# Differential attention: both maps' scores in one five-bank tile, a second transpose bank, and a third of each block's halves taken out of PSUM by ScalarE and VectorE

## The chip, the cores and the metric

The kernel runs on one core of one Trainium2 chip. The metric is the device time of one launch in microseconds, median of several runs. TensorE (PE) multiplies and transposes into PSUM, VectorE (DVE) and ScalarE (ACT) read PSUM and SBUF, GpSimd (POOL) works on SBUF here, and SyncE (SP) issues the DMAs. [...]

## The reference, cut to what matters

One step of a two-layer backbone. Layer 0 mixes tokens by differential attention: 8 heads, each with two maps of width 64, 1024 latent queries against 1280 keys (256 cached and 1024 new).

```
s = jnp.einsum('bqhmd,bkhmd->bhmqk', qi, k).astype(jnp.float32) * scale
p = jax.nn.softmax(s, axis=-1)
a = p[:, :, 0] - lam * p[:, :, 1]
return jnp.einsum('bhqk,bkhe->bqhe', a.astype(v.dtype), v)
```

The projections before it, the output projection, the feed-forward parts and all of layer 1 are as they were.

## The kernel before, in words

The changed part is the stage of latent differential attention, `diff_attention`, about 13% of the span. It works on 32 pairs: one head and two blocks of 128 queries. Every matrix product is made of halves (a rounded high part and the rest), so that fp32 accuracy comes out of three cheaper products. For a pair, with block i (0 or 1) and map m (0 or 1), a step is a method with one letter:

- S: six matmuls put a block's 128 x 1280 scores of one map into PSUM. R: VectorE's maximum over them. E: ScalarE's exponential of them, with their sum.
- c: two small VectorE operations on the sums of both maps. C: VectorE's combination `a` of both exponentials.
- T: transposes of `a`, in groups g of 4, 4 and 2 tiles of 128 keys. V: ScalarE copies a group from PSUM to SBUF (`a32`, two buffers). P: GpSimd rounds the copy to the high half and subtracts for the low half (`aT`).
- A: three matmuls of one tile of 128 keys with V into the accumulator, ten tiles for a pair. X, B, Y: the result is copied out, turned by two transposes and written to DRAM.
- W: a piece of the output projection's weights is split, in every second round (ScalarE, then VectorE).

The order is written out by hand: the string `ROUND` is run once for each pair, `DRAIN` once behind them. A token is letter, g or m, i, and how many rounds ago its pair began: `T201` is step T, group 2, block 0, of the pair before. Each engine runs its own instructions strictly in that order and waits where data or a buffer is missing; the framework puts in the waits, for a tile in PSUM bank by bank: two accesses of one tile by different engines to the same bank are put one behind the other, in the order of the text.

Before, a score tile takes three banks and there are two of them in turn; the transposes of T and B share one bank, and the accumulator has one.

Of the kernel before, what the change touches and what calls it, by code (L numbers as in the profile page):

```python
# [18 lines left out]
P = 128  # L19
# [25 lines left out]
def hybrid_step(ctx: ExitStack, tc: tile.TileContext, x_prompt, x_sample, cache_diff_k, cache_diff_v,  # L45
# [670 lines left out]
    def diff_attention(op, s1_all, wo_pool, pre, kv0, q0):  # L716
        NKB = NCB + 8
        NK = NKB * P
        with sbuf("da") as sb, psum("dap") as ps:
            class Pair:  # L720
# [9 lines left out]

                def step_S(self, m, i):

                    S = self.S[i, m] = ps.tile([P, 3 * 512], F32, name="S", tag="S", bufs=2)
                    for j in range(0, NK, 512):
                        n = min(NK - j, 512)
                        for f in range(2):
                            pe.matmul(S[:, j:j + n], lhsT=self.q[:, f, m, i * P:(i + 1) * P],  # L737
                                      rhs=kv[self.h][0][:, m, j:j + n], start=(f == 0), stop=(f == 1))

                def step_R(self, m, i):  # L740
                    if m == 0:
                        self.nm[i] = sb.tile([P, 2], F32, name="nm", tag="sm", bufs=8)
                        self.s2[i] = sb.tile([P, 2], F32, name="s2", tag="sm", bufs=8)
                    dve.tensor_reduce(out=self.nm[i][:, m:m + 1], in_=self.S[i, m][:, 0:NK], axis=AX.X, op=ALU.max,  # L744
                                      negate=True)

                def step_E(self, m, i):
                    e = self.e[i, m] = sb.tile([P, NK], F32, name="e", tag="e", bufs=4)
                    act.activation(out=e, in_=self.S[i, m][:, 0:NK], func=AF.Exp, bias=self.nm[i][:, m:m + 1],  # L749
                                   accum_out=self.s1(i) if m == 0 else self.s2[i][:, 0:1])  # L750

                def step_c(self, _, i):

                    r = self.s2[i][:, 1:2]
                    dve.reciprocal(out=r, in_=self.s2[i][:, 0:1])
                    dve.scalar_tensor_tensor(out=r, in0=self.s1(i), scalar=neglam, in1=r, op0=ALU.mult, op1=ALU.mult)

                def step_C(self, _, i):

# [3 lines left out]

                def step_T(self, g, i):

                    tp = self.tp[i, g] = ps.tile([P, 4, P], F32, name="tpa", tag="t", bufs=1)
                    for t in range(4 * g, min(4 * g + 4, NKB)):
                        pe.transpose(tp[:, t - 4 * g, :], self.a[i][:, t * P:(t + 1) * P], ident)

                def step_V(self, g, i):  # L770
                    n = min(4, NKB - 4 * g)
                    x = self.a32[i, g] = sb.tile([P, 4, P], F32, name="a32", tag="a32", bufs=2)
                    act.copy(out=x[:, 0:n, :], in_=self.tp[i, g][:, 0:n, :])  # L773

                def step_P(self, g, i):

                    n = min(4, NKB - 4 * g)
                    if g not in self.aT:
                        self.aT[g] = sb.tile([P, 2, 4 if g < 2 else 2, 2 * P], F32R, name="aT",
                                             tag="aT" if g < 2 else "aTb", bufs=4 if g < 2 else 2)  # L780
                    hi, lo = [self.aT[g][:, f, 0:n, i * P:(i + 1) * P] for f in range(2)]
                    x = self.a32[i, g][:, 0:n, :]
                    pool_round(hi, x)
                    (dve if self.last else pool).tensor_tensor(out=lo, in0=x, in1=hi.bitcast(F32), op=ALU.subtract)  # L784
# [16 lines left out]

                def step_B(self, _, __):

                    self.ot = ps.tile([P, 4, P], F32, name="tpo", tag="t", bufs=1)
                    for i in range(2):
                        pe.transpose(self.ot[:, i, :], self.oT[:, i * P:(i + 1) * P], ident)

                def step_Y(self, _, __):
# [2 lines left out]
                    t0 = self.tbs[0] * P  # L811
                    dma(out=o_d[t0:t0 + 2 * P, self.h * P:(self.h + 1) * P].rearrange("(t p) d -> p t d", p=P), in_=ot)

            pairs = [Pair(h, (tb, tb + 1)) for h in range(DH) for tb in range(0, 8, 2)]
            kv = {0: kv0}
            pairs[0].q = q0
# [2 lines left out]
            def wo_piece(i):  # L819
# [5 lines left out]

            ROUND = ("c001 A003 T012 A003 V202 V102 S000 R111 P213 T112 P002 A003 A003 E011 A003 P202 V012 "
                     "C001 P102 E111 T212 R000 V112 W000 S100 P012 R100 T001 X003 A002 V212 c011 E000 A002 "
                     "A002 B003 S010 V001 C011 Y003 T201 R010 A002 P112 E100 A002 T101 S110").split()  # L830


            DRAIN = ("c001 l1 A003 A003 V202 P213 l0 T012 V102 R111 A003 A003 P002 E011 P202 V012 A003 "
# [1167 lines left out]
```

## Time and profile before

| | |
|---|---|
| median of 3 runs | 3202.52 us (3199.64 to 3203.96) |
| the profiled execution, its own time | 3199.07 us |
| its span, first to last instruction | 3197.3 us |
| granted clock of TensorE, mean | 0.981 of full speed |
| busy share of the span | PE 94%, DVE 64%, ACT 44%, POOL 43% |
| the changed stage, first S to the last Y | about 387 to 818 us |

The profile's times count from the span's start. Matmuls overlap in TensorE's pipeline, so a busy share of PE is not a share of its peak. The profiled execution lies 3.45 us below the median of the runs.

### The profile page before, as it was taken

To read this page: it belongs to the slowest core of one execution; us is meant where nothing else is said; L and a number is where in the kernel's file an instruction comes from. 1 tells how busy PE (TensorE), PEld (TensorE's weight loads), DVE (VectorE), ACT (ScalarE), POOL (GpSimd) and SP (SyncE) were. 2 spreads that over 40 slices of the span, in tenths; PEclk is the share of its full clock that TensorE was granted. 3 is DMA by queue.
4 is the path that set the end of the run, shared out by engine and by line. 5 is a ranking of instruction groups with operands and counts; after the bars stand their busy time and mean duration, and the time that the engine had idled before them with its cause. 6 is when DMAs were issued, how large, how long until landed. Compare 5 with 4: busy or idle time off the path is not lost.

```text
span 3197.3 us, 47914 instructions
## 1 busy us (share of the span) xinstructions
PE 3001.8 (94%) x17998; PEld 2636.8 (82%) x17998; DVE 2048.6 (64%) x2789; ACT 1421.9 (44%) x2764; POOL 1361.9 (43%) x1186
## 2 busy tenths in 40 slices
PE   8999988998896999999999899999987999999999
PEld 5888777777776999999878787777767999998887
DVE  6786388888566777753786643999567633334544
ACT  6332267777554333333444323777433333333442
POOL 2553289999343444442021343666333433340101
PEclk9999999999998999999999999999988999999999
DMA  6675633332422434335765354433432322226564
GB/s 214 200 228 179 201 112 114 116 118 94 130 100 80 129 109 129 109 97 177 252 216 195 130 173 125 116 115 99 142 107 81 108 64 83 66 80 211 185 199 149
DMA packets 373808, 442.23 MB, mean 138 GB/s; under 512 B 26804, under 2 KB 295644, under 8 KB 373576
## 3 DMA queue, kind: packets, MB, share of 16 engines
q1 hardware_dynamic: 373576, 439.16, 43.6%
q8 instruction: 142, 2.33, 0.3%
q14 instruction: 90, 0.74, 0.1%
HBM read 335.71 MB, written 103.37 MB: 137 GB/s over the span
## 4 chain that ended last, share of the span: by engine, by line
PE 67%; POOL 14%; DVE 9%; ACT 4%; issue 3%; DMA 2%; SPq 1%; DVEq 0%; ACTq 0%; POOLq 0%
POOL aT L784 7%; PE guX L1518 6%; PE guX L1519 6%; PE guX L1520 6%; PE dacc L1635 5%; PE dacc L1637 5%; PE dacc L1636 5%; POOL aT L110 4%; PE qacc L556 4%; PE qacc L558 4%; PE qacc L557 4%; PE guY L1518 3%; PE guY L1520 3%; PE guY L1519 3%; PE guZ L1518 1%
## 5 line engine op out<-in xcount | busy, mean ns | idle before, releaser
L1551 POOL TENSOR_TENSOR sg<-sg,U 128x256 f32<-128x256 f32 x88 | 74.9, 851 | 563.4 <-ACT sg L1550 553.1
L1635 PE MATMUL dacc<-fh,ahl 128*128 128x512 f32 x792 | 312.0, 394 | 2.3 <-DVE U L1554 2.3
L1636 PE MATMUL dacc<-fl,ahl 128*128 128x512 f32 x792 | 310.7, 392 | 0.0
L1637 PE MATMUL dacc<-fh,ahl 128*128 128x512 f32 x792 | 310.7, 392 | 0.0
L556 PE MATMUL qacc<-whi,hh 128*128 128x512 f32 x648 | 259.7, 401 | 1.3 <-ACT hh L431 1.3
L558 PE MATMUL qacc<-whi,hl 128*128 128x512 f32 x648 | 254.9, 393 | 0.0
L557 PE MATMUL qacc<-wlo,hh 128*128 128x512 f32 x648 | 254.2, 392 | 0.6 <-DVE wlo L106 0.6
L154 POOL TENSOR_TENSOR xt<-yacc,xt 128x1024 f32<-128x1024 f32 (+1 forms) x19 | 49.7, 2621 | 459.9 <-DVE yacc L153 242.0
L784 POOL TENSOR_TENSOR aT<-a,aT 128x512 fp32r<-128x512 f32 x186 | 237.3, 1276 | 15.5
L1620 DVE TENSOR_TENSOR fl<-fraw,fh 128x1024 fp32r<-128x1024 f32 x132 | 165.4, 1253 | 121.3 <-ACT fh L1619 120.7
L744 DVE TENSOR_REDUCE nm<-S 128x1 f32<-128x1280 f32 x128 | 190.2, 1486 | 51.1 <-PE S L737 51.1
L1619 ACT CAST fh<-fraw 128x1024 fp32r<-128x1024 f32 x132 | 138.4, 1048 | 170.8 <-DMA fraw<-in_w_down_dram 156.7
L737 PE MATMUL S<-K,q 128*128 128x512 f32 (+1 forms) x768 | 184.5, 377 | 12.9 <-ACT e L749 8.9
L266 DVE SCALAR_TENSOR_TENSOR macc<-wmod,sc,macc 128x512 f32<-128x512 f32 x196 | 186.1, 992 | 0.0
L1635 PEld LDWEIGHTS dacc<-fh,ahl 128*128 128x128 f32 x792 | 149.2, 188 | 36.4 <-DVE U L1554 3.1
L1637 PEld LDWEIGHTS dacc<-fh,ahl 128*128 128x128 f32 x792 | 149.0, 188 | 33.7
L1636 PEld LDWEIGHTS dacc<-fl,ahl 128*128 128x128 f32 x792 | 149.1, 188 | 32.9
L749 ACT ACTIVATE e<-S,nm 128x1280 f32<-128x1280 f32 x128 | 171.4, 1339 | 7.2 <-DVE nm L744 7.1
L737 PEld LDWEIGHTS S<-K,q 128*128 128x128 f32 x768 | 137.5, 193 | 43.8 <-ACT e L749 19.0
L578 ACT CAST xT<-tpx 128x512 fp32r<-128x512 f32 x127 | 68.5, 592 | 236.5 <-issue 125.3
L110 POOL TENSOR_SCALAR aT<-a 128x512 fp32r<-128x512 f32 x192 | 154.0, 802 | 22.7 <-ACT a L773 22.7
L1490 DVE TENSOR_TENSOR fl<-fsum,fh 128x1024 fp32r<-128x1024 f32 x84 | 102.3, 1218 | 81.3 <-ACT fh L1488 81.3
(369 smaller groups left out, 9726.7 us busy)
## 6 DMA issues: line engine op xcount, KB each, us to landing
fraw<-in_w_down_dram SPq DMA_DIRECT2D x132, 512.0 KB
wmod<-in_w_mod_dram SPq DMA_DIRECT2D x112, 256.0 KB
araw<-a_d SPq DMA_DIRECT2D x132, 192.0 KB
fraw<-in_w_gate_dram SPq DMA_DIRECT2D x44, 512.0 KB
fraw<-in_w_up_dram SPq DMA_DIRECT2D x42, 512.0 KB
qT_d<-xT SPq DMA_DIRECT2D x36, 512.0 KB
q<-qT_d SPq DMA_DIRECT2D x64, 256.0 KB
wraw<-in_w_qkv_diff_dram SPq DMA_DIRECT2D x24, 512.0 KB
```

The source lines that it names most:

```text
L110: pool.tensor_scalar(out=out, in0=in_, scalar1=1.0, scalar2=0.0, op0=ALU.mult, op1=ALU.add)
L556: pe.matmul(acc, lhsT=xh, rhs=hi[:, a, :], start=(kb == 0), stop=False)
L557: pe.matmul(acc, lhsT=xh, rhs=lo[:, a, :], start=False, stop=False)
L558: pe.matmul(acc, lhsT=xl, rhs=hi[:, a, :], start=False, stop=(kb == KB - 1))
L737: pe.matmul(S[:, j:j + n], lhsT=self.q[:, f, m, i * P:(i + 1) * P], rhs=kv[self.h][0][:, m, j:j + n], start=(f == 0), stop=(f == 1))
L784: (dve if self.last else pool).tensor_tensor(out=lo, in0=x, in1=hi.bitcast(F32), op=ALU.subtract)
L1518: pe.matmul(o, lhsT=hi[:, kb, :], rhs=xh[:, kb, :], start=(first and kb == 0), stop=False, **more)
L1519: pe.matmul(o, lhsT=hi[:, kb, :], rhs=xl[:, kb, :], start=False, stop=False, **more)
L1520: pe.matmul(o, lhsT=lo[:, kb, :], rhs=xh[:, kb, :], start=False, stop=(kb == 3), **more)
L1635: pe.matmul(acc, lhsT=ah, rhs=hi[:, cs], start=(d == 0), stop=False)
L1636: pe.matmul(acc, lhsT=ah, rhs=lo[:, cs], start=False, stop=False)
L1637: pe.matmul(acc, lhsT=al, rhs=hi[:, cs], start=False, stop=(d == NDF - 1))
```

## The change

The score tile becomes one tile `scores` of five banks, made once: map 0 has its columns 0 to 1279, map 1 its columns 1280 to 2559. Map 0 fills banks 0 and 1 and half of bank 2; map 1 has the other half of bank 2 and banks 3 and 4. S cuts its matmuls at bank borders, still six. The bank that this frees goes to the transposes, which now have two. For the last group (g = 2, two of the ten tiles) V writes the high half straight from PSUM, and P becomes one VectorE subtraction out of PSUM; GpSimd does nothing for that group. The second operation of c becomes a `tensor_scalar`. `ROUND` and `DRAIN` are new orders.

```
                 def step_S(self, m, i):
-                    S = self.S[i, m] = ps.tile([P, 3 * 512], F32, name="S", tag="S", bufs=2)
-                    for j in range(0, NK, 512):
-                        n = min(NK - j, 512)
+                    j0 = m * NK
+                    S = self.S[i, m] = scores[:, j0:j0 + NK]
+                    cuts = [0] + [c - j0 for c in range(512, 5 * 512, 512) if j0 < c < j0 + NK] + [NK]
+                    for j, j1 in zip(cuts, cuts[1:]):
...
-                    dve.scalar_tensor_tensor(out=r, in0=self.s1(i), scalar=neglam, in1=r, op0=ALU.mult, op1=ALU.mult)
+                    dve.tensor_scalar(out=r, in0=r, scalar1=self.s1(i), scalar2=neglam, op0=ALU.mult, op1=ALU.mult)
...
-                    tp = self.tp[i, g] = ps.tile([P, 4, P], F32, name="tpa", tag="t", bufs=1)
+                    tp = self.tp[i, g] = ps.tile([P, 4, P], F32, name="tpa", tag="t", bufs=2)
...
+                def step_V(self, g, i):
...
+                    if g == 2:
+                        act.copy(out=self.halves(g, i)[0], in_=self.tp[i, g][:, 0:n, :])
+                        return
...
                 def step_P(self, g, i):
...
+                    if g == 2:
+                        dve.tensor_tensor(out=lo, in0=self.tp[i, g][:, 0:n, :], in1=hi.bitcast(F32), op=ALU.subtract)
+                        return
...
-                    self.ot = ps.tile([P, 4, P], F32, name="tpo", tag="t", bufs=1)
+                    self.ot = ps.tile([P, 4, P], F32, name="tpo", tag="t", bufs=2)
...
+            scores = ps.tile([P, 5 * 512], F32, name="S", tag="S", bufs=1)
...
-            ROUND = ("c001 A003 T012 A003 V202 V102 S000 R111 P213 T112 P002 A003 A003 E011 A003 P202 V012 "
-                     "C001 P102 E111 T212 R000 V112 W000 S100 P012 R100 T001 X003 A002 V212 c011 E000 A002 "
-                     "A002 B003 S010 V001 C011 Y003 T201 R010 A002 P112 E100 A002 T101 S110").split()
+            ROUND = ("E011 R111 A003 T012 C001 V112 V012 P102 S000 R000 P012 T212 E111 A003 A003 A003 S100 "
+                     "V212 P112 c011 A002 P212 X003 R100 C011 T001 E000 B003 A002 S010 Y003 R010 T101 V001 "
+                     "T201 E100 c000 W000 A002 A002 A002 S110 V101 V201 P201 A002 P001 T111").split()
```

What it does to each engine's order is shown at three places. A bracket behind a row names the engines whose signal the instruction waits for.

VectorE, one round of before (`nm` is R's result, two R for each buffer number: map 0, then map 1):

```order
L744 TENSOR_REDUCE nm_5871<-S_5889 128x1 [waits PE_49]
L761 SCALAR_TENSOR_TENSOR a_5951<-e_5879,s2_5810,e_5843 128x1280 [waits DVE_49]
L744 TENSOR_REDUCE nm_5961<-S_5917 128x1 [waits PE_49]
L744 TENSOR_REDUCE nm_5961<-S_5966 128x1 [waits PE_49]
L755 RECIPROCAL s2_5872<-s2_5872 128x1 [waits Activation_49]
L756 SCALAR_TENSOR_TENSOR s2_5872<-s1_all_3507,neglam_88,s2_5872 128x1 [waits DVE_49]
L761 SCALAR_TENSOR_TENSOR a_6011<-e_5956,s2_5872,e_5941 128x1280 [waits DVE_49]
L744 TENSOR_REDUCE nm_6019<-S_6002 128x1 [waits PE_49]
```

VectorE, one round of the change, from R111 to R010:

```order
L745 TENSOR_REDUCE nm_5025<-S_3517 128x1 [waits Activation_49]
L761 SCALAR_TENSOR_TENSOR a_5088<-e_5038,s2_4964,e_5008 128x1280 [waits DVE_49]
L745 TENSOR_REDUCE nm_5103<-S_3517 128x1 [waits PE_49]
L755 RECIPROCAL s2_5026<-s2_5026 128x1 [waits Activation_49]
L756 TENSOR_SCALAR s2_5026<-s2_5026,s1_all_3507,neglam_88 128x1 [waits DVE_49]
L791 TENSOR_TENSOR aT_5059<-tpa_5108,aT_5059 128x2x128 [waits Activation_49]
L745 TENSOR_REDUCE nm_5103<-S_3517 128x1 [waits PE_49]
L761 SCALAR_TENSOR_TENSOR a_5141<-e_5111,s2_5026,e_5077 128x1280 [waits DVE_49]
L745 TENSOR_REDUCE nm_5165<-S_3517 128x1 [waits PE_49,Activation_49]
```

The four R of a round waited for TensorE alone. The first row of the change, R111, waits for ScalarE. By the counts behind the signals that is E011, the exponential of the other map just ahead of it in `ROUND`. The subtraction from `tpa` is the new P.

ScalarE, one round of before (E000, E100, E011, E111; an `s1_all` among the outputs marks map 0):

```order
L749 ACTIVATE e_5991,s1_all_3507<-S_5917,nm_5961 128x1280 [waits DVE_49]
L773 COPY a32_6009<-tpa_5976 128x512 [waits PE_49,Activation_49,Pool_49]
L810 COPY ot_6013<-tpo_5999 128x256 [waits DMAHW7_49,PE_49]
L749 ACTIVATE e_6027,s2_5962<-S_5966,nm_5961 128x1280 [waits DVE_49]
L773 COPY a32_6065<-tpa_6016 128x256 [waits PE_49,Activation_49,Pool_49]
L773 COPY a32_6067<-tpa_6032 128x512 [waits PE_49,Activation_49,Pool_49]
L749 ACTIVATE e_6093,s1_all_3507<-S_6002,nm_6019 128x1280 [waits DVE_49]
L773 COPY a32_6101<-tpa_6057 128x512 [waits PE_49,Activation_49,Pool_49]
L749 ACTIVATE e_6108,s2_6020<-S_6037,nm_6019 128x1280 [waits DVE_49]
```

ScalarE, one round of the change, from E011 to E100:

```order
L749 ACTIVATE e_5077,s1_all_3507<-S_3517,nm_5025 128x1280 [waits PE_49,Activation_49]
L784 COPY a32_5090<-tpa_5068 128x512 [waits PE_49,Activation_49,Pool_49]
L784 COPY a32_5092<-tpa_5083 128x512 [waits PE_49,Activation_49,Pool_49]
L749 ACTIVATE e_5111,s2_5026<-S_3517,nm_5025 128x1280 [waits DVE_49]
L781 CAST aT_5059<-tpa_5108 128x2x128 [waits PE_49]
L811 COPY oT_5138<-av_4993 128x256 [waits PE_49]
L749 ACTIVATE e_5148,s1_all_3507<-S_3517,nm_5103 128x1280 [waits DVE_49]
L821 COPY ot_5162<-tpo_5150 128x256 [waits DMAHW6_49,PE_49]
L784 COPY a32_5173<-tpa_5143 128x512 [waits Activation_49,Pool_49]
L749 ACTIVATE e_5178,s2_5104<-S_3517,nm_5103 128x1280 [waits DVE_49]
```

Every E waited for VectorE, for its own map's R. Now the first row, E011, waits for TensorE, and by the counts that is S110, the scores of the other map. E111 waits for R000, E000 for R100 and E100 for R010, by the counts; each of these R reads the other map, and E's own R is older.

TensorE around S000, before:

```order
L768 MATMUL tpa_5905<-ident_71,a_5863 128x128 x3
L793 MATMUL av_5835<-aT_5801,V_4842 128x256
L794 MATMUL av_5835<-aT_5801,V_4842 128x256
L795 MATMUL av_5835<-aT_5801,V_4842 128x256
L737 MATMUL S_5917<-K_5444,q_5744 128x512 [waits DMAHW0_49,Activation_49]
L737 MATMUL S_5917<-K_5444,q_5744 128x512 [waits DMAHW2_49,DMAHW1_49]
L737 MATMUL S_5917<-K_5444,q_5744 128x512 x2
L737 MATMUL S_5917<-K_5444,q_5744 128x256 x2
```

TensorE around S000, of the change, to the first matmuls behind it:

```order
L768 MATMUL tpa_5083<-ident_71,a_5001 128x128 [waits DVE_49]
L768 MATMUL tpa_5083<-ident_71,a_5001 128x128 x3
L738 MATMUL S_3517<-K_4789,q_4933 128x512 [waits DMAHW7_49,DVE_49]
L738 MATMUL S_3517<-K_4789,q_4933 128x512 [waits DMAHW1_49,DMAHW0_49]
L738 MATMUL S_3517<-K_4789,q_4933 128x512 x2
L738 MATMUL S_3517<-K_4789,q_4933 128x256 x2
L768 MATMUL tpa_5108<-ident_71,a_5001 128x128 [waits Activation_49]
L768 MATMUL tpa_5108<-ident_71,a_5001 128x128
```

S000 waited for ScalarE (the exponential that read this buffer last) and its loads. Now it waits for VectorE, by the counts R111, which reads the other map.

## Rows read from the trace of the kernel before

**Rows 1.** Stretch, length, busy us (instructions) of PE, PEld, DVE, ACT, POOL; clock, DMA.

```profile
412.00:794.00 382.00, 342.99 (x2263) 298.75 (x2264) 331.84 (x316) 271.58 (x494) 366.65 (x359) 1.00 0.35 109
```

**Rows 2.** Timeline, a round in the middle: start, length, engine, line, operation.

```profile
562.19 1.41 PE L737 MATMUL S<-K,q 128*128 128x512 f32 x6
...
563.63 1.49 DVE L744 TENSOR_REDUCE nm<-S 128x1 f32<-128x1280 f32 x1 [0.74 <-PE S L737]
...
564.75 1.29 POOL L784 TENSOR_TENSOR aT<-a,aT 128x512 fp32r<-128x512 f32 x1
...
565.04 2.34 DVE L761 SCALAR_TENSOR_TENSOR a<-e,s 128x1280 f32<-128x1280 f32 x1
...
571.61 0.40 POOL L110 TENSOR_SCALAR aT<-a 128x256 fp32r<-128x256 f32 x1
...
571.69 1.66 DVE L761 SCALAR_TENSOR_TENSOR a<-e,s 128x1280 f32<-128x1280 f32 x1
...
575.21 1.42 PE L737 MATMUL S<-K,q 128*128 128x512 f32 x6
```

**Rows 3.** Who waited for whom, 387 to 800 us: total, times, longest.

```profile
ACT a L773 <- POOL aT L784: 83.1, 91, 2.2
DVE nm L744 <- PE S L737: 51.1, 79, 1.8
PEld tpa L768 <- ACT a L773: 28.3, 58, 1.3
PEld tpo L806 <- ACT a L773: 25.1, 29, 1.1
```

**Rows 4.** Single lines: shortest, median and longest instruction in ns, first and last start.

```profile
L761 DVE SCALAR_TENSOR_TENSOR a<-e,s x64: 1540/2120/2660, 400.5 to 798.1; 128x1280 f32<-128x1280 f32 x64
L773 ACT COPY a<-tpa x192: 362/585/592, 405.3 to 811.2; 128x512 f32<-128x512 f32 x128, 128x256 f32<-128x256 f32 x64
L110 POOL TENSOR_SCALAR aT<-a x192: 404/617/1873, 406.0 to 811.7; 128x512 fp32r<-128x512 f32 x128, 128x256 fp32r<-128x256 f32 x64
L784 POOL TENSOR_TENSOR aT<-a,aT x186: 725/1287/2393, 406.7 to 803.0; 128x512 fp32r<-128x512 f32 x124, 128x256 fp32r<-128x256 f32 x62
L784 DVE TENSOR_TENSOR aT<-a,aT x6: 424/687/692, 805.1 to 812.4; 128x512 fp32r<-128x512 f32 x4, 128x256 fp32r<-128x256 f32 x2
```

**Rows 5.** Timeline, the start of the stage.

```profile
386.96 2.59 PE L737 MATMUL S<-K,q 128*128 128x512 f32 x12 [0.73 <-ACT qout L601]
...
399.86 4.53 PE L737 MATMUL S<-K,q 128*128 128x512 f32 x12 [0.78 <-ACT e L749]
...
402.39 1.49 DVE L744 TENSOR_REDUCE nm<-S 128x1 f32<-128x1280 f32 x1 [0.33 <-PE S L737]
403.98 1.33 ACT L749 ACTIVATE e<-S,nm 128x1280 f32<-128x1280 f32 x1 [1.92 <-DVE nm L744]
...
405.45 1.44 PE L737 MATMUL S<-K,q 128*128 128x512 f32 x6 [0.63 <-ACT e L749]
...
409.21 1.48 DVE L744 TENSOR_REDUCE nm<-S 128x1 f32<-128x1280 f32 x1
...
410.72 1.33 ACT L749 ACTIVATE e<-S,nm 128x1280 f32<-128x1280 f32 x1 [1.62 <-DVE nm L744]
...
412.19 1.19 PE L737 MATMUL S<-K,q 128*128 128x512 f32 x4 [2.13 <-ACT e L749]
```

**Rows 6.** Timeline, the last S of the stage and the last C.

```profile
792.35 1.40 PE L737 MATMUL S<-K,q 128*128 128x512 f32 x6
...
798.15 2.58 DVE L761 SCALAR_TENSOR_TENSOR a<-e,s 128x1280 f32<-128x1280 f32 x1
```

**Rows 7.** Busy time and granted clock, columns as in rows 1, three stretches.

```profile
404.00:414.00 10.00, 6.60 (x39) 5.13 (x37) 9.47 (x10) 7.36 (x12) 7.38 (x7) 1.00 0.26 76
798.00:799.00 1.00, 0.38 (x1) 0.19 (x1) 0.90 (x2) 0.00 (x0) 0.92 (x2) 1.00 0.00 0
800.00:801.00 1.00, 1.00 (x6) 1.00 (x6) 0.84 (x2) 0.91 (x6) 1.00 (x1) 0.50 0.00 0
```

More of the change, by code (lines that the diff above doesn't have):

```diff
@@ L731, in step_S @@
                 def step_S(self, m, i):
-                    S = self.S[i, m] = ps.tile([P, 3 * 512], F32, name="S", tag="S", bufs=2)
-                    for j in range(0, NK, 512):
-                        n = min(NK - j, 512)
+                    j0 = m * NK
+                    S = self.S[i, m] = scores[:, j0:j0 + NK]
+                    cuts = [0] + [c - j0 for c in range(512, 5 * 512, 512) if j0 < c < j0 + NK] + [NK]
+                    for j, j1 in zip(cuts, cuts[1:]):
                         for f in range(2):
-                            pe.matmul(S[:, j:j + n], lhsT=self.q[:, f, m, i * P:(i + 1) * P],
-                                      rhs=kv[self.h][0][:, m, j:j + n], start=(f == 0), stop=(f == 1))
+                            pe.matmul(S[:, j:j1], lhsT=self.q[:, f, m, i * P:(i + 1) * P],
+                                      rhs=kv[self.h][0][:, m, j:j1], start=(f == 0), stop=(f == 1))
                 def step_R(self, m, i):
@@ L743, in step_R @@
                         self.s2[i] = sb.tile([P, 2], F32, name="s2", tag="sm", bufs=8)
-                    dve.tensor_reduce(out=self.nm[i][:, m:m + 1], in_=self.S[i, m][:, 0:NK], axis=AX.X, op=ALU.max,
-                                      negate=True)
+                    dve.tensor_reduce(out=self.nm[i][:, m:m + 1], in_=self.S[i, m], axis=AX.X, op=ALU.max, negate=True)
                 def step_E(self, m, i):
                     e = self.e[i, m] = sb.tile([P, NK], F32, name="e", tag="e", bufs=4)
-                    act.activation(out=e, in_=self.S[i, m][:, 0:NK], func=AF.Exp, bias=self.nm[i][:, m:m + 1],
+                    act.activation(out=e, in_=self.S[i, m], func=AF.Exp, bias=self.nm[i][:, m:m + 1],
                                    accum_out=self.s1(i) if m == 0 else self.s2[i][:, 0:1])
@@ L764, in step_T, with halves @@
                 def step_T(self, g, i):
-                    tp = self.tp[i, g] = ps.tile([P, 4, P], F32, name="tpa", tag="t", bufs=1)
+                    tp = self.tp[i, g] = ps.tile([P, 4, P], F32, name="tpa", tag="t", bufs=2)
                     for t in range(4 * g, min(4 * g + 4, NKB)):
                         pe.transpose(tp[:, t - 4 * g, :], self.a[i][:, t * P:(t + 1) * P], ident)
+                def halves(self, g, i):
+                    n = min(4, NKB - 4 * g)
+                    if g not in self.aT:
+                        self.aT[g] = sb.tile([P, 2, 4 if g < 2 else 2, 2 * P], F32R, name="aT",
+                                             tag="aT" if g < 2 else "aTb", bufs=4 if g < 2 else 2)
+                    return [self.aT[g][:, f, 0:n, i * P:(i + 1) * P] for f in range(2)]
                 def step_V(self, g, i):
                     n = min(4, NKB - 4 * g)
+                    if g == 2:
+                        act.copy(out=self.halves(g, i)[0], in_=self.tp[i, g][:, 0:n, :])
+                        return
                     x = self.a32[i, g] = sb.tile([P, 4, P], F32, name="a32", tag="a32", bufs=2)
@@ L777, in step_P @@
                     n = min(4, NKB - 4 * g)
[L778 to L781, printed above, removed]
+                    hi, lo = self.halves(g, i)
+                    if g == 2:
+                        dve.tensor_tensor(out=lo, in0=self.tp[i, g][:, 0:n, :], in1=hi.bitcast(F32), op=ALU.subtract)
+                        return
                     x = self.a32[i, g][:, 0:n, :]
@@ L823, in wo_piece @@
                 wsplit(raw, wo[kb][0][:, cs], wo[kb][1][:, cs])
-            ROUND = ("c001 A003 T012 A003 V202 V102 S000 R111 P213 T112 P002 A003 A003 E011 A003 P202 V012 "
-                     "C001 P102 E111 T212 R000 V112 W000 S100 P012 R100 T001 X003 A002 V212 c011 E000 A002 "
-                     "A002 B003 S010 V001 C011 Y003 T201 R010 A002 P112 E100 A002 T101 S110").split()
-            DRAIN = ("c001 l1 A003 A003 V202 P213 l0 T012 V102 R111 A003 A003 P002 E011 P202 V012 A003 "
[3 rows of a table removed]
-                     "A001 A001 A001 A001 P211 A001 A001 A001 n0 s11 X001 B001 Y001 n1").split()
+            ROUND = ("E011 R111 A003 T012 C001 V112 V012 P102 S000 R000 P012 T212 E111 A003 A003 A003 S100 "
+                     "V212 P112 c011 A002 P212 X003 R100 C011 T001 E000 B003 A002 S010 Y003 R010 T101 V001 "
+                     "T201 E100 c000 W000 A002 A002 A002 S110 V101 V201 P201 A002 P001 T111").split()
+            DRAIN = ("E011 R111 A003 T012 C001 V112 V012 P102 P012 T212 E111 A003 A003 A003 V212 P112 c011 "
[3 rows of a table added]
+                     "Y001 s10 n0 s11 n1").split()
             n = len(pairs)
```

6 rows, old and new, of the table DRAIN are left out of this document.

## The prediction

> **What bounds the stage now.** I read the busy time of the stage first, then the waits, then the timeline of one round and of the start. In 382 us POOL is busy 366.65, PE 342.99, DVE 331.84 and ACT 271.58 [rows 1]. From one S to the same S a round later it takes 575.21 - 562.19 = 13.02 us [rows 2]; so a round holds 12.50 us of POOL, 11.69 of PE, 11.31 of DVE and 9.26 of ACT. The longest total among the waits is ScalarE's V on GpSimd's subtraction, 83.1 us in 91 waits: the two `a32` buffers are full. TensorE's transposes wait for the V behind that, 28.3 and 25.1 us [rows 3]. The reader is to see one bound, GpSimd's halves, with its wait handed on to ScalarE and TensorE. VectorE waits 51.1 us for scores [rows 3], so no engine has much room.
>
> **What the change takes away.** The last group leaves GpSimd: twice a rounding (0.404) and a subtraction (0.725, the shortest of each line are the 256-wide ones) [rows 4], 2.26 us a round, which leaves 10.24. ScalarE's work stays one pass for the group. VectorE gets two subtractions of 256 columns at 0.424 [rows 4]; that row read SBUF, no row here reads PSUM at this width, so 0.4 to 0.7 each: 0.8 to 1.4 a round. The second operation of c may give back 0.2 to 0. The second transpose bank removes the 53.4 us of waits above, if V comes in time. Were that all, a round would be VectorE's 11.31 + 0.85 = 12.16 us.
>
> **What it adds: one chain through bank 2.** Both maps have part of bank 2, and the framework keeps the engines apart there. The order rows show it: R111 waits for ScalarE where every R waited for TensorE, E011 waits for TensorE where every E waited for VectorE, S000 waits for VectorE. With the counts named behind those rows, a round is one ring of twelve instructions, each waiting for the one ahead:
>
> S000, R000, E111, S100, R100, E000, S010, R010, E100, S110, E011, R111, and S000 of the next round.
>
> Before, each map had its own ring of S, R, E, twice a round, and the two overlapped. Now scores, maximum and exponential never run at the same time.
>
> The links, start to start:
> - S to what reads it: 563.63 - 562.19 = 1.44 [rows 2].
> - R to E: 410.72 - 409.21 = 1.51 and 403.98 - 402.39 = 1.59, E having been idle [rows 5]; I take 1.55.
> - E to S: 405.45 - 403.98 = 1.47 and 412.19 - 410.72 = 1.47 [rows 5].
>
> Nine links are of these kinds. S110 to E011, E011 to R111 and R111 to S000 are handed to another engine than in any row; their bounds are the instruction's own length (1.41, 1.33, 1.49) below and some 0.15 more than my values above; I take the values, as for the same giver with another reader. Ring: 4 x (1.44 + 1.55 + 1.47) = 17.84 us.
>
> C001 stands between R111 and R000 on VectorE's queue. R000 could start 1.55 + 1.44 = 2.99 after R111; behind C it starts after 1.49 plus C. C takes 1.66 when a short GpSimd rounding had just begun (571.61, 571.69), and 2.34 when a subtraction had (564.75, 565.04) [rows 2]; its ends are 1.54 and 2.66 [rows 4]. That adds 0.04 to 1.16. V112 and V012 (0.59 each [rows 4]) follow E011, and R111 follows it too, for 1.49; so P012's rounding begins some 0.3 us ahead of C001, nearest the 1.66 row: +0.16. **A round: 18.0 us.**
>
> The rest fits beside the ring. TensorE's other work, 11.69 less four S of 1.41, is 6.1 us a round; `ROUND` spreads it over the four gaps of 4.46 - 1.44 = 3.0 between one S and the next. ScalarE has 9.26 - 4 x 1.33 = 3.9 beside its E, in the same four gaps, and GpSimd 10.2 in 18. VectorE has four R (5.96), two C (about 3.8) and 12.16 less these, 2.4 us, for both c, W and both P; c000, W and P201 are the most that stand together, some 2 us from E100's end, and R111 is due 4.38 - 1.33 = 3.05 us from there. C011 has the 2.9 us of E000 and S010. The DMAs are the same, a whole round ahead of their use. So the removed waits, GpSimd's 2.26 us and VectorE's extra 0.85 all disappear under the ring; were the ring gone, they would be the difference between 13.02 and 12.16.
>
> **The sum.** From the first S000 to the last S110 it took 792.35 - 386.96 = 405.4 us [rows 5, 6]. Now: 31 rounds at 18.0 = 558.0; in the last round S000 to S110 are three times 4.46 = 13.4; round 0 has no E111, -1.5. TensorE idles most of round 0, and its clock falls there as it did before: a cold S to R takes 402.39 - 399.86 = 2.53, 1.09 more [rows 5]. Only rounds 1 and 2 bring it transposes and A; I charge 8 cold S, +8.7 (bounds 2 and 12). That is 578.6, so +173.2. Behind the last S110 the chain to the last C was 798.15 + 2.58 - 792.35 = 8.4 us [rows 6]; now it is 1.44 + 1.47 + 1.55 + 1.47, then c (0.4 to 0.7) and C (1.66 to 2.58): 8.0 to 9.2. DRAIN loads and squares the first output blocks later; I add 2 (0 to 4). The profiled execution took 3199.07: 3199.1 + 175 = **3374 us**; against the median of the runs, 3202.52, that is 5.4% more.
>
> [...] The order rows alone give the 18.0. [...]
>
> **The rivals.**
>
> 1. *Faster.* The ring's waits cost little, because what they wait for is mostly done, and the freed GpSimd and the second transpose bank show. For it: the 83.1 and 53.4 us of waits are real, and the change removes their cause. Against: it decides below 13.02 us a round, and the ring would have to lose 5 us, more than three of its twelve links; each link's giver is the instruction just ahead of it in `ROUND`. Time: 31 x (13.02 - 12.16) = 27 less, 3172. [...]
>
> 2. *The clock falls in mid-stage.* TensorE would work some 11 us in 18, with pauses of 1.5 to 2 us. For it: after the thin stretch at 796 to 800 (0.38 busy) the clock was at half [rows 7]. Against: at 404 to 414, 6.6 of 10 us busy, with a pause of 2.13 us, it stayed full [rows 5, 7]. If every second S is cold: 62 x 1.09 = +68, 3441; all of them, 3509.
>
> 3. *A queue adds a wait to the ring.* P201 must end before R111; it needs V201, which stands behind W and V101 on ScalarE, and V101 needs P012's buffer. The room is about 0.9 us. If that is gone, 1 to 2 us a round: 3405 to 3436.
>
> 4. *The chain is there, but the bank waits are partly met early,* so that a round is 13 to 15 us: 3199 to 3260.
>
> **How the numbers follow.** A measurement of this kernel can tell about 0.2%, 6 us. Forecast, a ring of 17.6 to 18.7 us: 3353 (31 x 17.6 + 13.4 - 1.5 + 2 = 559.5, +154) to 3403 (31 x 18.7, 12 cold S, 4 behind: +204); chance 0.68. Rival 2: 0.14. Rival 3: 0.10. Rival 1: 0.05. Rival 4: 0.03, a third of it within 6 us. The range that leaves out the faster cases and the coldest clock is 3345 to 3440, about 8 in 10. Slower 0.94, same 0.01, faster 0.05.
>
> **What would show it.** Right: the same S twice 18 us apart; R waiting for S at nearly every S, E waiting for R, S waiting for E; V waiting for POOL in few places; every engine under 70% busy in the stage; R111 starting behind E011, never beside it. C at 1.6 to 1.9 in one of its two places. Wrong: R of one map running beside E of the other; a round of 12 to 13 us; half clock within 430 to 900 us; VectorE waiting at P201.

## The result and the profile after

The changed kernel takes 3372.18 us (median of 4 runs, 3369.8 to 3373.57), the kernel before 3202.15 us beside it: a ratio of 1.0531, 95% interval 1.0513 to 1.0549, slower. The profiled execution of the change took 3369.8 us, its span is 3368.0 us, 170.7 longer than before.

The page first: busy time of each engine, then three groups of the stage (busy us, mean ns of one, idle time of the engine just before them and what ended it).

```profile
PE 3027.7 (90%) x17998; PEld 2656.4 (79%) x17998; DVE 2042.6 (61%) x2851; ACT 1417.8 (42%) x2764; POOL 1250.4 (37%) x1060
...
L738 PE MATMUL S<-K,q 128*128 128x512 f32 (+1 forms) x768 | 194.8, 391 | 196.9 <-ACT e L749 146.6
...
L749 ACT ACTIVATE e<-S,nm 128x1280 f32<-128x1280 f32 x128 | 170.0, 1328 | 305.6 <-DVE nm L745 285.5
...
L745 DVE TENSOR_REDUCE nm<-S 128x1 f32<-128x1280 f32 x128 | 190.9, 1492 | 139.7 <-PE S L738 86.8
```

S and E in the kernel before:

```profile
L737 PE MATMUL S<-K,q 128*128 128x512 f32 (+1 forms) x768 | 184.5, 377 | 12.9 <-ACT e L749 8.9
...
L749 ACT ACTIVATE e<-S,nm 128x1280 f32<-128x1280 f32 x128 | 171.4, 1339 | 7.2 <-DVE nm L744 7.1
```

PE's share fell from 94% to 90%. S, R and E last about what they lasted; new is what stands behind the last bar: E found ScalarE idle for 305.6 us (7.2 before), nearly all of it until an R ended, and S found TensorE idle for 196.9 us (12.9 before), mostly until an E ended. Who waited for whom from 387 to 965 us (total, times, longest) answers to [rows 3]:

```profile
POOL aT L110 <- ACT a L784: 305.2, 91, 29.3
ACT e L749 <- DVE nm L745: 282.5, 94, 6.9
...
PE S L738 <- ACT e L749: 145.2, 94, 3.1
...
DVE nm L745 <- PE S L738: 86.8, 67, 4.1
...
DVE nm L745 <- ACT e L749: 49.8, 31, 2.8
PE S L738 <- DVE nm L745: 46.6, 31, 1.6
ACT e L749 <- PE S L738: 19.2, 31, 2.1
```

The waits of before are gone: no V waits for GpSimd, no transpose for a V. In their place S, R and E wait for one another, and GpSimd waits 305.2 us for work. The counts matter more than the sums: three times a round E waits for R, three times S for E, twice R for S (the third R follows C without a gap, below), and once each of R for E, S for R and E for S. The last three, which the kernel before does not have, are handed on from one map to the other. One round, S110 to the next S110 (timeline, as [rows 2]):

```profile
606.14 1.43 PE L738 MATMUL S<-K,q 128*128 128x256 f32 x6 [1.39 <-ACT e L749]
...
607.67 1.33 ACT L749 ACTIVATE e<-S,nm 128x1280 f32<-128x1280 f32 x1 [0.83 <-PE S L738]
...
609.12 1.49 DVE L745 TENSOR_REDUCE nm<-S 128x1 f32<-128x1280 f32 x1 [1.83 <-ACT e L749]
...
610.52 1.56 DVE L761 SCALAR_TENSOR_TENSOR a<-e,s 128x1280 f32<-128x1280 f32 x1
...
610.66 1.44 PE L738 MATMUL S<-K,q 128*128 128x512 f32 x6 [1.50 <-DVE nm L745]
...
610.84 2.40 POOL L795 TENSOR_TENSOR aT<-a,aT 128x512 fp32r<-128x512 f32 x1
...
612.14 1.49 DVE L745 TENSOR_REDUCE nm<-S 128x1 f32<-128x1280 f32 x1
...
613.67 1.33 ACT L749 ACTIVATE e<-S,nm 128x1280 f32<-128x1280 f32 x1 [3.62 <-DVE nm L745]
...
615.14 1.43 PE L738 MATMUL S<-K,q 128*128 128x256 f32 x6 [1.75 <-ACT e L749]
...
616.60 1.49 DVE L745 TENSOR_REDUCE nm<-S 128x1 f32<-128x1280 f32 x1 [0.69 <-PE S L738]
...
618.13 1.33 ACT L749 ACTIVATE e<-S,nm 128x1280 f32<-128x1280 f32 x1 [2.51 <-DVE nm L745]
...
619.60 1.45 PE L738 MATMUL S<-K,q 128*128 128x512 f32 x6 [1.67 <-ACT e L749]
...
621.16 1.49 DVE L745 TENSOR_REDUCE nm<-S 128x1 f32<-128x1280 f32 x1 [1.60 <-PE S L738]
...
622.68 1.33 ACT L749 ACTIVATE e<-S,nm 128x1280 f32<-128x1280 f32 x1 [2.38 <-DVE nm L745]
...
624.15 1.44 PE L738 MATMUL S<-K,q 128*128 128x256 f32 x6 [1.38 <-ACT e L749]
```

The starts of S, R and E follow one another in the twelve steps of the forecast: E011 1.53 us behind S110, R111 1.45 behind it, S000 1.54, then R000 1.48, E111 1.53, S100 1.47, R100 1.46, E000 1.53, S010 1.47, R010 1.56, E100 1.52, and S110 1.47: 18.01 us. None begins before the one ahead of it has ended. Busy time and clock of the stage (columns as in [rows 1]):

```profile
440.00:962.00 522.00, 350.60 (x2196) 304.21 (x2194) 314.55 (x363) 257.42 (x476) 249.98 (x230) 0.97 0.25 79
```

In these 522 us PE is busy 67%, DVE 60%, ACT 49%, POOL 48%; no engine is the limit. The first S (granted clock 1.00), the first S at reduced clock (a "cold" S; the granted clock is 0.57 from 389.68 to 391.94 us) and the last S:

```profile
386.67 1.43 PE L738 MATMUL S<-K,q 128*128 128x512 f32 x6 [0.73 <-ACT qout L601]
...
389.68 2.26 PE L738 MATMUL S<-K,q 128*128 128x256 f32 x6 [1.58 <-DVE nm L745]
```

```profile
967.97 1.44 PE L738 MATMUL S<-K,q 128*128 128x256 f32 x6 [1.38 <-ACT e L749]
```

From the first S to the last it takes 967.97 - 386.67 = 581.3 us, where it was 405.4 [rows 5, 6].

### The profile page after: what moved, and what is told of

Same layout as the page of the kernel before. It is cut to its first block, busy times and chain, and to the rows that moved or that the text cites. A ratio compares the mean times of both kernels' runs of the same rounds, so it can differ in the third digit from the quotient of the medians.

```text
span 3368.0 us, 47843 instructions
## 1 busy us (share of the span) xinstructions
PE 3027.7 (90%) x17998; PEld 2656.4 (79%) x17998; DVE 2042.6 (61%) x2851; ACT 1417.8 (42%) x2764; POOL 1250.4 (37%) x1060
## 4 chain that ended last, share of the span: by engine, by line
PE 53%; DVE 8%; ACT 3%; issue 2%; POOL 2%; DMA 1%; SPq 0%; DVEq 0%; ACTq 0%; POOLq 0%
PE guX L1531 5%; PE guX L1532 5%; PE guX L1533 5%; PE dacc L1648 5%; PE dacc L1650 5%; PE dacc L1649 5%; PE guY L1533 3%; PE guY L1531 3%; PE guY L1532 3%; PE guZ L1531 1%; PE guZ L1533 1%; PE guZ L1532 1%; PE qacc L556 1%; PE qacc L558 1%; PE qacc L557 1%
## 5 line engine op out<-in xcount | busy, mean ns | idle before, releaser
L738 PE MATMUL S<-K,q 128*128 128x512 f32 (+1 forms) x768 | 194.8, 391 | 196.9 <-ACT e L749 146.6
L749 ACT ACTIVATE e<-S,nm 128x1280 f32<-128x1280 f32 x128 | 170.0, 1328 | 305.6 <-DVE nm L745 285.5
L795 POOL TENSOR_TENSOR aT<-a,aT 128x512 fp32r<-128x512 f32 x124 | 193.1, 1557 | 10.4
L110 POOL TENSOR_SCALAR aT<-a 128x512 fp32r<-128x512 f32 x128 | 80.7, 631 | 311.1 <-ACT a L784 311.0
```

Source lines behind the costliest of these rows:

```text
L738: pe.matmul(S[:, j:j1], lhsT=self.q[:, f, m, i * P:(i + 1) * P], rhs=kv[self.h][0][:, m, j:j1], start=(f == 0), stop=(f == 1))
```

## The experiments

Two questions: is it the ring, and what makes the ring. Ratios are against the kernel before, run beside each. "Round" below is the mean time from an E to the same E a round later, from the starts of E between 490 and 790 us. In most kernels with two score tiles two lengths alternate, 13.0 and 12.57 us in the kernel before, 12.79 on average (W stands in every second round). In the change it is 18.0 us in most rounds and 18.1 on average.

### Two score tiles again

The change, with scores and transposes laid out as before; order, halves and c stay the change's.

```
-                    S = self.S[i, m] = scores[:, j0:j0 + NK]
+                    S = self.S[i, m] = ps.tile([P, 3 * 512], F32, name="S", tag="S", bufs=2)
...
-                    tp = ... name="tpa", tag="t", bufs=2)
+                    tp = ... name="tpa", tag="t", bufs=1)
...
-... C011 T001 E000 B003 A002 S010 Y003 R010 T101 V001 T201 ...
+... C011 T001 E000 V001 B003 A002 S010 Y003 R010 T101 T201 ...
```

> The change with the scores back in two three-bank tiles and one transpose bank; the halves of the last group, the operation of c and the new order stay (only V001 stands earlier, behind E000's matmuls, since one bank cannot hold two groups). Ring theory: no bank has both maps any more, so the ring of twelve falls apart into one of S, R and E for each score tile, twice a round (8.9 us); the next limit is VectorE's 12.2 us of work or the single transpose bank, a round of 12.2 to 14.5 us, 3172 to 3245 us, and R of one map beside E of the other in the timeline. Rival, the new order or VectorE's added work sets the round: it stays near 18 us, 3340 to 3400 us.

3205.29 us, ratio 1.0019 (1.0007 to 1.003). The loss is gone but for 0.2% of the time, with the new order and VectorE's added work still in place. The timeline shows an exponential with a maximum of another score tile beside it:

```profile
604.20 1.33 ACT L748 ACTIVATE e<-S,nm 128x1280 f32<-128x1280 f32 x1
...
604.81 1.49 DVE L744 TENSOR_REDUCE nm<-S 128x1 f32<-128x1280 f32 x1 [0.42 <-PE S L737]
```

A round takes 13.23 us here, not the 12.2 that VectorE's sum would allow, and no engine is the limit: from 500 to 780 us TensorE is busy 239.25 of 280 us, VectorE 223.80 and GpSimd 190.72. What holds the round at 13.23 us was not isolated.

### The new order alone

The kernel before with `ROUND` and `DRAIN` of the change (and two tokens moved, as one transpose bank and two buffers need it).

```
-            ROUND = ("c001 A003 T012 A003 V202 V102 S000 R111 P213 T112 P002 A003 A003 E011 A003 P202 V012 "
+            ROUND = ("E011 R111 A003 T012 C001 V112 V012 P102 S000 R000 P012 T212 E111 A003 A003 A003 S100 "
...
```

> The kernel before with the new order alone (V001 moved ahead of B003 and P201 behind P001, as one transpose bank and two buffers need it): two score tiles, all halves by GpSimd, the old c. Ring theory: the order costs little by itself; GpSimd's 12.5 us a round stays the bound and the order fits it worse than its own, 3200 to 3270 us. Rival, the order makes the loss: 3340 us or more.

3221.48 us, ratio 1.0065 (1.0044 to 1.0085), a round of 13.43 us. The order costs 0.6% by itself; it doesn't make the loss. Beside the run with two score tiles, which has the same order and also one transpose bank, it shows something more: the new halves and the new c together take 3221.48 to 3205.29 us, a gain of 0.5%.

### The five-bank tile alone

```
-                    S = self.S[i, m] = ps.tile([P, 3 * 512], F32, name="S", tag="S", bufs=2)
+                    S = self.S[i, m] = scores[:, j0:j0 + NK]
...
-... S000 R111 P213 T112 P002 A003 A003 E011 A003 ...
+... R111 P213 T112 P002 A003 A003 E011 S000 A003 ...
```

> The kernel before with nothing but the five-bank score tile (one transpose bank, all halves by GpSimd, the old operation of c, the old order but S000 moved from ahead of R111 to behind E011, because one tile cannot hold two blocks of a map). Ring theory: the text gives a ring of twelve again (R111, E011, S000, E111, R000, S100, R100, E000, S010, R010, E100, S110), 17.9 us and up to 1 us more where C stands ahead of a link: 3365 to 3430 us, and GpSimd is no longer the bound. Rival, the order or VectorE's added work is the cause: neither is in this kernel, 3195 to 3230 us.

3531.94 us, ratio 1.1031 (1.0974 to 1.1088). The tile alone does the harm, and more of it than the whole change: rounds of 22.3 to 24.9 us, at least 100 us above the forecast. The ring was there, but longer than the forecast had it. Its timeline from 500 to 780 us shows where: from an E to the S that waits for it 2.1 to 2.5 us twice a round and 3.1 to 4.1 us once, where the change has 1.47; the granted clock is 0.84 in this stretch, for 0.97 in the change. It has one transpose bank, and the runs with one further down show what that does to a ring; the five-bank tile in the old order with two wasn't run.

### Which part of the scores a maximum reads

Two kernels, in which each maximum covers only half of the keys, so that the exponentials take another offset. In the first the half contains the shared bank 2, in the second it lies outside it.

```
-                    dve.tensor_reduce(out=..., in_=self.S[i, m], axis=AX.X, op=ALU.max, negate=True)
+                    dve.tensor_reduce(out=..., in_=self.S[i, m][:, 640 - 640 * m:1280 - 640 * m], ...)
```

and for the second kernel `[:, 640 * m:640 + 640 * m]`.

> The change, but each maximum reads half of the keys only, 640 columns, so that the exponentials take another offset: for map 0 columns 640 to 1279 and for map 1 columns 0 to 639 of its scores, which contain the shared bank 2. Ring theory: R stays in the ring and is about 0.7 us shorter, four times a round: 18.0 - 2.7 = 15.3 us, 31 rounds less 83 us, 3280 to 3300 us. Rival, VectorE's load or its queue sets the round: VectorE has the same relief here as with the other half, so both give the same time.

> The change, but each maximum reads the other half of the keys: for map 0 columns 0 to 639 and for map 1 columns 640 to 1279 of its scores, which lie outside the shared bank 2; the number of columns, and so VectorE's work, is that of the run before. Ring theory: no R has to wait for the other map or hold it back; eight links of S and E remain, 4 x (1.44 to 1.55 + 1.47) = 11.6 to 12.1 us, about what TensorE has to do in a round (11.7): a round of 12 to 13 us, 3185 to 3220 us. Rival, VectorE's load or its queue: the time of the run with the half on bank 2, about 3290 us.

3283.68 us (ratio 1.0255, 1.0226 to 1.0285) and 3283.93 us (1.0256, 1.0226 to 1.0286): the same. The first is what the ring gave, 15.33 us a round for 15.3 forecast. The second refutes the theory as it was put: R has no column in bank 2, and yet it waits as often and as long as in the first. R's wait for the other map's E from 387 to 870 us, first kernel, then second:

```profile
DVE nm L745 <- ACT e L749: 49.8, 31, 2.8
```

```profile
DVE nm L745 <- ACT e L749: 49.8, 31, 2.8
```

The rival's condition is met too, equal times. But it is not VectorE's load that acts: in the stretch from 500 to 780 us VectorE is busy 150.00 of 280 us in the second kernel. Nor is it VectorE's queue: the six-bank kernel of the next section has the work and the order of the run with two score tiles, and takes 334 us more. What is left is a ring that doesn't ask for the bank.

### One tile of six banks, and one transpose bank

Three kernels tell the tile from the bank. The first gives each map three banks of its own, but in one tile; the second is the change with one transpose bank; the third the change with only the moved V001.

```
-                    j0 = m * NK
+                    j0 = m * 3 * 512
...
-            scores = ps.tile([P, 5 * 512], F32, name="S", tag="S", bufs=1)
+            scores = ps.tile([P, 6 * 512], F32, name="S", tag="S", bufs=1)
```

(first kernel; it and the second also have `tag="t", bufs=1`, and all three V001 ahead of B003.)

> As the run with two three-bank tiles, but the scores are one tile of six banks, map 0 in its banks 0 to 2 and map 1 in its banks 3 to 5, so that no bank has both maps; everything else is the same. After the run with half a maximum off bank 2 two readings are left. By bank: the ring needs the shared bank, and this run goes like the one with two tiles, a round of about 13 us, 3195 to 3225 us. By tile: the framework puts accesses of different engines to one PSUM tile one behind the other whatever their banks; the ring of twelve is whole, 18.0 us, 3365 to 3400 us with the single transpose bank.

> The change (one five-bank score tile) with a single transpose bank and V001 ahead of B003. It stands between the change and the run with one six-bank tile. If the ring belongs to the tile and not to a bank, five or six banks make no difference: 3525 to 3555 us, as the six-bank tile, and the second transpose bank is worth some 168 us inside the ring, because with one bank a T waits for a V that stands behind an E of the ring, and the S behind that T waits with it. If the six-bank tile was slow for a reason of its own: about 3372 to 3400 us.

> The change with V001 moved ahead of B003 and nothing else, two transpose banks: the move that the runs with one transpose bank needed. If it costs nothing, and the single bank all of the 168 us: 3365 to 3380 us. If the move itself delays an E of the ring (V001 then stands between E000 and E100 as before, only ahead of Y003): up to 0.6 us a round, 3390 us.

Six banks: 3539.55 us (1.1058, 1.1036 to 1.108). Five banks: 3533.54 us (1.1038, 1.1016 to 1.106). V001 moved, two transpose banks: 3374.66 us (1.0541, 1.052 to 1.0563). Busy time from 500 to 780 us in the same order:

```profile
500.00:780.00 280.00, 176.64 (x903) 150.13 (x904) 129.85 (x150) 109.12 (x196) 100.80 (x96) 0.84 0.21 64
```

```profile
500.00:780.00 280.00, 172.87 (x908) 147.95 (x906) 129.05 (x151) 110.38 (x198) 100.32 (x96) 0.86 0.21 65
```

```profile
500.00:780.00 280.00, 187.56 (x1173) 162.68 (x1172) 168.78 (x194) 138.24 (x256) 135.64 (x125) 0.97 0.28 86
```

First, banks of its own for each map give nothing as long as both are in one tile; in two tiles the same six banks gave 3205.29 us. So the framework puts the engines' accesses to a PSUM tile in line by tile. What is said of it ahead of the prediction, bank by bank, is wrong for this program. Whether the chip would need those waits wasn't tried. Secondly, neither forecast for the six-bank run was right (3365 to 3400 by tile); those for the other two were. The single transpose bank adds 3533.54 - 3374.66 = 159 us, some 5 us a round. The timeline of the second kernel shows how:

```profile
602.67 2.34 PE L738 MATMUL S<-K,q 128*128 128x512 f32 x6
...
606.64 1.33 ACT L749 ACTIVATE e<-S,nm 128x1280 f32<-128x1280 f32 x1 [4.00 <-DVE nm L745]
...
607.96 0.57 ACT L784 COPY a<-tpa 128x512 f32<-128x512 f32 x1
...
608.59 0.55 PE L768 MATMUL tpa<-ident,a 128*128 128x128 f32 x2 [2.90 <-ACT a L784]
...
610.86 1.94 PE L738 MATMUL S<-K,q 128*128 128x256 f32 x6
...
612.90 1.33 ACT L749 ACTIVATE e<-S,nm 128x1280 f32<-128x1280 f32 x1 [3.35 <-PE S L738]
```

Behind the first E, ScalarE's queue holds a V (607.96), the transposes of the next group wait for its bank (608.59), and three tiles of A and then S stand behind the transposes in TensorE's queue (610.86). From E to that S it takes 610.86 - 606.64 = 4.22 us instead of 1.47, and every instruction of the ring behind it is late by the difference. The S at 602.67 is late in the same way, 2.90 us behind its E (599.77). The granted clock, 0.86 in this stretch for 0.97, adds its part: it was 0.50 from 602 to 605 us and 0.66 from 610.9 to 612.8, the two S took 2.34 and 1.94 us instead of 1.43, and their readers start 2.45 and 2.04 us behind them instead of some 1.55. In this round of 23.58 us the two late S make 4.2 us of the excess and the clock 1.4.

### What GpSimd's relief is worth without the ring

Four kernels with two score tiles and the old order, but for a few tokens that the halves or subtractions need moved. The first has the change's V and P (P behind its V, since the one bank is held until P has read it) and its c:

```
+                    if g == 2:
+                        act.copy(out=self.halves(g, i)[0], in_=self.tp[i, g][:, 0:n, :])
+                        return
...
+                    if g == 2:
+                        dve.tensor_tensor(out=lo, in0=self.tp[i, g][:, 0:n, :], in1=hi.bitcast(F32), op=ALU.subtract)
+                        return
```

> The kernel before with the last group's halves out of PSUM by ScalarE and VectorE and the new operation of c alone: two score tiles, one transpose bank, the old order (P of the last group stands right behind its V, since one bank is held until P has read it). GpSimd falls to 10.2 us a round, VectorE rises to 12.2. Theory that this part of the change was good and the tile undid it: a round of 12.2 to 13.0 us, 3170 to 3200 us. Rival, VectorE's subtraction or the longer hold of the transpose bank costs as much as GpSimd's relief gives: 3200 to 3240 us.

3272.32 us, ratio 1.0225 (1.0208 to 1.0242): dearer than either side said. The timeline, behind a maximum on VectorE:

```profile
602.86 1.49 DVE L744 TENSOR_REDUCE nm<-S 128x1 f32<-128x1280 f32 x1 [1.30 <-PE S L737]
...
603.28 0.37 ACT L781 CAST aT<-tpa 128x256 fp32r<-128x256 f32 x1
...
604.65 0.41 DVE L791 TENSOR_TENSOR aT<-tpa,aT 128x256 fp32r<-128x256 f32 x1
...
605.12 0.66 PE L768 MATMUL tpa<-ident,a 128*128 128x128 f32 x4 [1.36 <-DVE aT L791]
```

ScalarE has the high half at 603.28 + 0.37, but VectorE's queue holds R (602.86) and c in front of the subtraction, which comes at 604.65; only then is the bank free for the next transposes, at 605.12. From 500 to 780 us TensorE's transposes wait 24.1 us for such subtractions, and 36.4 us more are put down to the c just ahead of one. Before, the bank came free with the V. The granted clock adds its part: 0.95 in this stretch for 1.00 before. So in the old order this part of the change costs 2.2%. The single bank alone is not to blame: in the new order, with one bank, the same halves and c gained 0.5% (above). What a second transpose bank would give here was not shown: beside two score tiles of three banks and the accumulator's it would be the ninth bank, and no kernel here lays out more than eight at a time.

The other three leave V and the rounding as before and move only subtractions, out of SBUF, to VectorE: of block 1 behind C011 (`if g == 2 and i == 1`), of both blocks (block 0 between c001 and R111; the diff), and of both with a third buffer (its last two lines).

```
                     pool_round(hi, x)
-                    (dve if self.last else pool).tensor_tensor(out=lo, in0=x, ...)
+                    if g == 2:
+                        self.q2 = lambda lo=lo, x=x, hi=hi: dve.tensor_tensor(out=lo, in0=x, ...)
+                        return
...
-                    x = self.a32[i, g] = sb.tile([P, 4, P], F32, name="a32", tag="a32", bufs=2)
+                    x = self.a32[i, g] = sb.tile([P, 4, P], F32, name="a32", tag="a32", bufs=3)
```

> The kernel before, old order, two score tiles, V and GpSimd's rounding as before; only the subtraction of the last group of block 1 goes to VectorE, out of SBUF, behind C011 where VectorE then waited 0.6 us for scores. GpSimd's share of it was 1.85 us there, because C ran beside it. GpSimd 12.5 - 1.85 + 0.3 to 0.7 (the stretch falls on the next instruction) = 11.0 to 11.7, VectorE 11.31 + 0.42 = 11.7, TensorE 11.69: a round of 11.9 to 12.7 us, 3165 to 3195 us. Rival, the round is held by the hand-overs of scores and the one transpose bank rather than by GpSimd's sum: 3195 to 3205 us.

> As the run before, and the subtraction of the last group of block 0 on VectorE too, between c001 and R111. GpSimd 10.5 to 11.2 us a round, VectorE 12.16, which is then the bound: a round of 12.2 to 12.9 us, 3172 to 3200 us; slower than with one subtraction moved if VectorE's sum decides, the same if the hand-overs do.

> As the run with both subtractions on VectorE, and a third a32 buffer. In that run GpSimd was busy 11.0 of 13.12 us a round and yet the round was no shorter, and ScalarE's V still waited for a subtraction to give back one of the two buffers (43.3 us in 280). Theory that this loop of V, rounding, subtraction and buffer sets the round: with a third buffer V no longer waits for GpSimd, the one transpose bank comes free earlier, VectorE's 12.16 us is the next bound, a round of 12.2 to 12.8 us, 3172 to 3192 us. Rival, the wait for the buffer is only where the slack lies, and the round is set by the one transpose bank and the hand-overs between T, V, S and R: 3198 to 3207 us.

3205.13 us (1.0013, 1.0004 to 1.0023), 3206.53 us (1.0017, 1.0008 to 1.0026) and 3199.72 us (0.9998, 0.9989 to 1.0007). None beats the kernel before. Busy time from 500 to 780 us of the three:

```profile
500.00:780.00 280.00, 243.53 (x1644) 215.24 (x1642) 231.07 (x246) 201.42 (x357) 250.52 (x237) 1.00 0.36 111
```

```profile
500.00:780.00 280.00, 242.82 (x1640) 214.64 (x1638) 239.67 (x269) 200.70 (x355) 234.81 (x216) 1.00 0.35 111
```

```profile
500.00:780.00 280.00, 246.17 (x1657) 218.53 (x1658) 272.27 (x272) 199.31 (x362) 230.08 (x219) 1.00 0.35 111
```

With rounds of 13.02, 13.02 and 12.86 us, GpSimd is busy 11.65, 10.92 and 10.57 us of a round (250.52 / 280 x 13.02, and so on), where it was 12.29 before (269.06 of 280 us, at 12.79), and the round is no shorter. (The 13.12 us in the expectation is the longer of two lengths.) In the second the wait of V for GpSimd stays:

```profile
ACT a L773 <- POOL aT L788: 43.3, 64, 1.0
```

The third buffer takes it away, as its theory said; the round still doesn't follow, and the time is that of the rival. VectorE is now busy 272.27 of 280 us, because C takes longer. C, in the second and then in the third:

```profile
L761 DVE SCALAR_TENSOR_TENSOR a<-e,s 128x1280 f32<-128x1280 f32 x43 | 67.6, 1572 | 0.7
```

```profile
L761 DVE SCALAR_TENSOR_TENSOR a<-e,s 128x1280 f32<-128x1280 f32 x44 | 98.7, 2242 | 0.8
```

C's mean is 0.67 us higher with the third buffer. GpSimd's instructions stand beside it in both kernels, but otherwise in time: in the second kernel every C takes 1.54 to 1.66 us, and begins ahead of GpSimd's instruction, just behind the start of a short rounding or near the end of a subtraction; in the third half of them begin together with a subtraction and take 2.7 us. So the buffer's wait was real. That VectorE is the limit without it, at about the old round, is a reading from its busy time; no run took load from VectorE.

## Why the prediction was right, and where it was not

The time was forecast at 3374 and is 3372.18. The reason, one ring of twelve, was right but for its condition, the shared bank. That the figures agree to 2 us is luck in part: errors cancel in the links and again in the sum.

- **What bounds the stage now.** The reading that GpSimd's halves are the one bound fell. In the old order, taking 0.6 to 1.7 us a round from GpSimd gave nothing; in the new order the change's halves with its c gave 0.5%. The likely picture is a balance: of the 12.79 us of a mean round before, GpSimd was busy 12.3, TensorE 11.5 and VectorE 11.1 (500 to 780 us), with the hand-overs through one transpose bank and two buffers between them. Which of these holds the round was not shown one by one. The 12.16 us that the prediction names for a round without the ring, and rival 1's 3172 us with it, were reached by no run: 13.23 us and 3205.29 without the ring. And 13.02 is the longer of two alternating rounds; at the mean, 12.79, the loads of a round come out 2% lower. The forecast's sum doesn't rest on it.
- **What the change takes away.** P out of PSUM took 0.42 us, the lower end; the second operation of c 0.27 instead of 0.36. GpSimd is at 249.98 / 522 x 18.0 = 8.6 us a round, not 10.2. Most of that gap is a price: the prediction took the shortest subtraction of 256 columns, 0.725 us, for both, but in the kernel before only one of the two took that; the other ran into C and took 1.85 us. The mean of both is 1.29 us (second line below, 500 to 780 us of the kernel before), so what left GpSimd was 2 x (0.41 + 1.29) = 3.4 us a round, not 2.26. None of it reaches the end.

```profile
L110 POOL TENSOR_SCALAR aT<-a 128x512 fp32r<-128x512 f32 x88 | 86.6, 984 | 0.0
L784 POOL TENSOR_TENSOR aT<-a,aT 128x256 fp32r<-128x256 f32 x44 | 56.9, 1293 | 3.7
```

- **One chain.** Right in each of its twelve links, and shown: two tiles in place of one give the loss back but for 0.2% of the time. "Through bank 2" is the part that failed: the halves off bank 2 and the six-bank tile show that the tile makes the chain, whatever the banks.
- **The links.** 18.01 us for 18.0, from errors that cancel. S to its reader is 1.46 to 1.56 for 1.44, 0.27 more over the four; the other eight links take 0.10 less; and the 0.16 for C001 was not met. C001 ends at 610.52 + 1.56 = 612.08, and R000 starts at 612.14, just behind S000's end (610.66 + 1.44 = 612.10); C began 0.32 us ahead of GpSimd's subtraction, and the subtraction was the longer one (2.40 us, for 1.27 at 613.91 with no C beside it).
- **The rest fits beside the ring.** Right for this layout, and incomplete: that the gain of the second transpose bank disappears under the ring holds against the kernel before, but without that bank the ring is some 5 us longer.
- **The sum.** The profiled execution grew by 170.7 us, for 175. The stage grew to 581.3 us, 2.7 more than forecast. Up to 437 us eight S were cold (2.26 to 2.50 us; granted clock 0.58 from 389.6 to 437.0 us, 0.50 from 437.40 to 439.90), as charged; short dips of the clock later are the likely remainder (the five below; mean 0.97 from 440 to 962 us). From the last S to the first matmul of the output projection it takes 998.27 - 967.97 = 30.3 us for 820.65 - 792.35 = 28.3, the 2 us of DRAIN. Not forecast: the change is 177.6 us late at the output projection's start, but 171.5 at the first transposes of the prompt part (1038.74 - 867.26). In between, TensorE waited 4.7 us for GpSimd in the kernel before, and its clock was 0.88 from 840 to 868 us; in the change that wait is missing in this part, and the clock was 0.93 from 998 to 1018 us and then 1.00. Whether DRAIN's other order causes that wasn't tried.
- **The rivals.** The clock fell in mid-stage only in short dips, not at every second S. Five S of mid-stage took over 1.6 us: 1.71, 2.20, 1.89, 1.88 and 1.75 us (at 488, 560, 669, 850 and 904 us), and while they ran the granted clock was 0.79, 0.59, 0.70, 0.70 and 0.77. Another, at 437.40, was cold (2.50 us). So half clock within 430 to 900 us, which the prediction names as a sign of being wrong, did appear (0.50 from 437.40 to 439.90 us and from 560.8 to 561.6); by the growth of the stage it cost some 3 us. P201 added no wait. The waits were not met early in any round: from 490 to 790 us none is shorter than 17.9 us. C took 1.54 and 1.56 us in its two places, not the 1.6 to 1.9 expected in one.

## What to carry to other kernels

Count what one PSUM tile couples: here the framework orders all engines' accesses to a tile, so two independent streams that share a tile become one ring, whatever banks they use. Two tiles in place of one took 5% off the change, though they left one bank less for the transposes, and 9% off the kernel with one tile of six banks. And before an engine's load is taken for the bound of a stage, take some of it away: here an engine was busy 96%, and relieving it by 5 to 14% made no round shorter. What a relief is worth also hangs on the order: under the new one the halves gave 0.5%, under the old one they cost 2.2%.

## What the runs showed of the hardware

From 500 to 780 us of the change C took 1.54 us in the 15 places where no GpSimd instruction ran beside it. Where one did, in the kernel before and in the change, the one that clearly began second took longer. In [rows 2] GpSimd's subtraction was 0.29 us ahead and C took 2.34 us; after the change C was 0.32 us ahead (1.56 us) and the subtraction took 2.40, for 1.27 at 613.91 with no C beside it. With a rounding it was the same: in the kernel before, the one that began at 566.00, while C ran, took 1.86 us, and in the change the mean of such roundings is 0.62 us. Where the two began 0.04 us apart, the order of the starts did not tell it: with the third buffer C started first and took 2.69 us, the subtraction 1.30. Why one of the two takes longer was not taken apart.

```profile
610.58 2.69 DVE L761 SCALAR_TENSOR_TENSOR a<-e,s 128x1280 f32<-128x1280 f32 x1
610.62 1.30 POOL L788 TENSOR_TENSOR aT<-a,aT 128x512 fp32r<-128x512 f32 x1
```

So GpSimd's and VectorE's loads of a round changed with the order. From the kernel before to the change, 500 to 780 us, the mean of C goes from 2.00 to 1.55 us and that of GpSimd's 512-wide rounding from 0.98 to 0.62, while its 512-wide subtraction goes from 1.29 to 1.57.
